# Maxima over the partitions: a GpSimd all-reduce replaced by a trip through DRAM and a VectorE reduction

## The chip, the cores and the metric

The kernel runs on one core of a Trainium2 chip. The metric is the device time in microseconds (us). TensorE does the matrix products (the profile's PE, and PEld for its weight loads), VectorE (DVE), ScalarE (ACT) and GpSimd (POOL) the elementwise work, SyncE (SP) issues DMAs. Each takes its instructions in the order in which they were written; they wait for each other through semaphores.

## The reference

One inference step of a two-layer trunk, for a prompt of 16 + 1024 tokens and eight running sequences of one token each, 1048 columns in all. Cut to what matters here:

```python
def trunk(x, ...):                       # D_MODEL 1024, D_FF 4096
    for i in range(2):
        h = rms_norm(x, norm_mix_pre[i])
        m = ssd_mixer(h, ...) if i == 0 else rglru_mixer(h, ...)
        x = x + rms_norm(m, norm_mix_post[i])
        h = rms_norm(x, norm_ffn_pre[i])
        x = x + rms_norm(sq_relu_mlp(h, w1[i], w2[i]), norm_ffn_post[i])

def ssd_mixer(u, ...):                   # 32 heads of 64 in 8 groups, state 128
    z, xbc, dt = split(u @ w_in)         # 1024 x 6176
    xbc = silu(causal_conv(xbc))         # 4 taps
    y, h = ssd_chunked(...)              # chunks of 128: decay matrix, carried state
    return group_rms_norm((y + D * x) * silu(z)) @ w_out

def rglru_mixer(u, ...):
    gate, xr = split(u @ w_in + b_in)    # 1024 x 2048
    h = scan(a, b)                       # a, b from sigmoids of block products of conv(xr)
    return (h * gelu(gate)) @ w_out + b_out

def sq_relu_mlp(x, w1, w2):
    return relu(x @ w1) ** 2 @ w2
```

All in float32.

## The kernel before, in words

Channels lie on the partitions and the 1048 columns along the free dimension, in pieces of 350, 350 and 348. Each float32 product is made of float16 products: an operand is scaled by a power of two and split into a high and a low half, and three products hi x hi, hi x lo, lo x hi add up in PSUM.

**Weight strips.** The weights come in strips of 128 x 2048 float32 (1 MB; 256 output channels over all 1024 inputs). `load_strip` (L537) has SyncE load a strip into `ws`, which has two buffers. `wconv` (L565) finds the largest magnitude in each partition, `rm` (128x1): with VectorE (L581, L602) or, for the strips of kind "a" in the SSD stage, as a sum of magnitudes with ScalarE (L579). `strip_scale` (L542) makes the maximum over the 128 partitions, in every partition, `wgb`, and from it the power of two (`qw`, `pw`, `sw`, in `pow2`, L529 to L533) and its inverse `winv` (L548). Then `split` (L551) writes the halves: ScalarE the high one (L558), VectorE the low one (L562), into `wh` (five buffers). For strips of kinds "H" and "S", in the FFNs, `sums` makes combinations `wp` as well (L640, L641) and GpSimd forms differences in `ws` in place (L648). 105 strips are scaled on `rm` or its like and four more on `gmx`, maxima taken earlier (L583).

**Stages.** From 100 to 990 us of the profiled execution, the SSD stage: eight groups, and for each the projection of the next one on TensorE (L742, evacuated by ScalarE: `pre` at L1150 and L1155, `z` at L1249) between nine chunk steps (`tp`, L1284; `st`, L1327; `yo`, L1331 and L1335). In each chunk the state goes through GpSimd (`hst`, L1344, times a decay) and VectorE (L1345, plus the new part), GpSimd adds to `yf` (L1352), and the group's norm adds squares there (`gsq`, L1435). SyncE loads the decay factors `L` (L1294) and `ex` (L1299) for each chunk. Then the output projection; from 1190 the first FFN, in Strassen-like units (`unit`, L1618: the products `mm` of L677, added up in `z` by VectorE at L1634 to L1645 and in `acc` at L1565, split into `H` at L1516 or L1598); from 1800 the LRU stage; from 2230 the second FFN.

**Order.** The body writes the program as interleaved generators. After that `Order` builds the graph of all instructions, runs a list schedule over it with a length for each instruction (`Order.length`, L122 on), four rounds forward and back, keeps the best, and pins every engine, SyncE included, to that order. The length of a partition all-reduce stands there as 600 ns.

Of the kernel before, what the change touches and what calls it, by code (L numbers as in the profile page):

```python
# [12 lines left out]
F32 = mybir.dt.float32  # L13
# [3 lines left out]
OP = mybir.AluOpType  # L17
AX = mybir.AxisListType
PSUM = bass.MemoryType.PSUM
DRAM = bass.MemoryType.DRAM  # L20
RED = bass.bass_isa.ReduceOp
EXPSET = "natural_log_exp_and_others"

P = 128
# [55 lines left out]
class Order:  # L80
# [40 lines left out]
    @staticmethod  # L121
    def length(i, kind, outs, ins):  # L122

        n = max([int(np.prod([x[1] for x in list(a.ap)[1:]] or [1])) for a in outs + ins] or [1])
        scal = sum(all(x[1] == 1 for x in list(a.ap)[1:]) for a in ins)
        eng = str(i.engine).split(".")[-1]
        if kind == "InstLoadActFuncSet":
            return 20
        if kind == "InstDMACopy":
            return 350 if eng == "SP" else 600  # L130
        if eng == "PE":
            c = int(np.prod([x[1] for x in list(outs[0].ap)[1:]]))
            if ins[0].dtype == F32:
                t = 2 * max(110, c / 1.2 + 2)
                return t / 2 if tuple(i.tile_size)[1] < 128 else t
            return max(30, c / 2.4 + 2.2)
        if eng == "DVE":
            if kind == "InstReciprocal":
                return 150 + 6 * n
            if "InstTensorScalarPtr" == kind and i.is_tensor_tensor_scan:  # L140
                return 150 + 2.08 * n
            return 65 + n / 0.96 + 65 * min(scal, 2) * (n > 1) + 80 * (len(outs) > 1)
        if eng == "Activation":
            return 90 + 0.83 * n + 90 * scal + 190 * (len(outs) > 1)
        if kind == "InstPartitionAllReduce":
            return 600
        if kind == "InstTensorTensor":
            return 200 + 2.19 * n
        return 110 + 6 * n if kind == "InstTensorCopy" else 110 + n
# [255 lines left out]
class Body:  # L405
# [26 lines left out]
    def setup(self):  # L432
        nc, tc, ctx = self.nc, self.tc, self.ctx
        self.const = ctx.enter_context(tc.tile_pool(name="const", bufs=1))
        self.tiny = ctx.enter_context(tc.tile_pool(name="tiny", bufs=3))
        self.upool = ctx.enter_context(tc.tile_pool(name="u", bufs=1))
        self.ws = ctx.enter_context(tc.tile_pool(name="ws", bufs=2))
        self.wh = ctx.enter_context(tc.tile_pool(name="wh", bufs=5))
# [30 lines left out]
        gb = c.tile([P, 5], F32, name="gb")  # L469
# [18 lines left out]
        self.yd = [self.dram.tile([P, 4 * NV], F16, name=f"yd{i}") for i in range(G)]  # L488
        self.csd = self.dram.tile([288, P], F32, name="csd")
        self.esd = self.dram.tile([288, P], F32, name="esd")  # L490
        self.bcd = [self.dram.tile([8, 2, P], F32, name=f"bcd{i}") for i in range(2)]
        self.mad = [self.dram.tile([P, KT * w], F32, name=f"mad{c}") for c, w in enumerate(WC)]
        a = self.a
# [46 lines left out]
        return st  # L540

    def strip_scale(self, gmax):  # L542
        nc, ty = self.nc, self.tiny
        gb = ty.tile([P, 1], F32, tag="wgb", name="wgb")
        nc.gpsimd.partition_all_reduce(gb, gmax, P, RED.absmax)  # L545
        s, p = self.pow2(gb, 1, ty, "w")
        inv = ty.tile([P, 1], F32, tag="winv", name="winv", bufs=8)
        nc.vector.tensor_scalar(inv, p, 2.0 ** -14, None, op0=OP.mult)  # L548
        return s, inv, gb
# [1382 lines left out]
```

## Time and profile before

| what | value |
|---|---|
| time, median of 3 runs | 2951.6 us (2949.22 to 2952.95) |
| profiled execution | 2956.49 us; span from first to last instruction 2954.8 us |
| granted TensorE clock, mean | 0.950 |
| DMA traffic | 237.73 MB, mean 80 GB/s |
| POOL instructions | 1036 |

In lines of groups, `L545 POOL PARTITION_ALL_REDUCE wgb<-rm x105 | 49.8, 475 | 728.9 <-issue 358.3` reads: line 545, engine, operation, tile written and read, 105 of them, 49.8 us busy in all, 475 ns each, 728.9 us of idle time of the engine just before them, of which "issue" (a wait for nothing that the profile shows) ended 358.3 us. In lines of waits, the engine with its tile and line stands left of the arrow, what it waited for right of it, then us in total, how often, and the longest. In lines in order of time: start, length, engine, line, operation, tiles, shapes, and in brackets the engine's idle time before it and what ended that.

### The profile page before, as it was taken

Reading aid. Unit: us, or ns where it says so; the run is one execution under the profiler, and the core shown is the slowest. Engines: PE = TensorE matmul, PEld = TensorE weight load, DVE = VectorE, ACT = ScalarE, POOL = GpSimd, SP = SyncE. Lnnn points to the kernel's source line nnn. Section 1 sums busy time; section 2 is a strip of 40 time slices with the busy share of each in tenths; the row PEclk is TensorE's granted clock in tenths of the full one; section 3 lists DMA queues with packets and bytes.
Section 4 is the critical chain, followed back from the end, with each engine's and each line's share of the span. In section 5 each row is a group of like instructions: output and inputs, shape, how many; then the busy total and the mean of one; then the engine's idle time right before and its main releaser. Section 6 shows DMA issues by size and latency. Waiting matters only on the chain.

```text
span 2954.8 us, 57301 instructions
## 1 busy us (share of the span) xinstructions
PE 2585.9 (88%) x23193; PEld 2048.1 (69%) x23193; DVE 2089.2 (71%) x4682; ACT 1408.2 (48%) x2436; POOL 764.0 (26%) x1036
## 2 busy tenths in 40 slices
PE   4979889788888998977988899998999879979898
PEld 2656556555555565876988896665667868979886
DVE  4757557656754477676878778896885677778786
ACT  4556455555654345334335144577664335244252
POOL 2222222222222102353232210122112652241211
PEclk9999999899898999998999999999999989999999
DMA  3232333133235522010112112310230011111122
GB/s 123 76 112 80 121 115 116 68 132 103 79 118 182 201 88 68 30 44 30 59 44 87 58 58 97 140 38 33 83 136 30 30 44 44 44 44 44 45 84 91
DMA packets 71498, 237.73 MB, mean 80 GB/s; under 512 B 11120, under 2 KB 37152, under 8 KB 50368
## 3 DMA queue, kind: packets, MB, share of 16 engines
q1 hardware_dynamic: 64848, 199.35, 19.5%
q0 software_dynamic: 6384, 34.71, 3.1%
q8 instruction: 181, 2.97, 0.4%
q14 instruction: 85, 0.70, 0.1%
HBM read 194.67 MB, written 39.36 MB: 79 GB/s over the span
## 4 chain that ended last, share of the span: by engine, by line
DVE 25%; PE 21%; issue 15%; POOL 7%; ACT 4%; DMA 2%; SPq 0%; POOLq 0%; DVEq 0%; ACTq 0%
PE mm L742 17%; DVE wh L562 4%; DVE wp L641 3%; PE mm L677 2%; POOL ws L648 2%; DVE z L1636 2%; DVE z L1640 1%; POOL f L1594 1%; DVE acc L1565 1%; DMA ws<-w 1%; POOL f L1609 1%; DVE z L1637 1%; DVE r L596 1%; DVE H L1516 1%; DVE z L1643 1%
## 5 line engine op out<-in xcount | busy, mean ns | idle before, releaser
L742 PEld LDWEIGHTS <-wh 128*128 128x128 f16 x8832 | 863.3, 99 | 546.7 <-issue 90.0
L742 PE MATMUL mm<-U,wh 128*128 128x350 f16 (+1 forms) x5760 | 912.1, 319 | 74.2 <-ACT z L1249 42.4
L677 PEld LDWEIGHTS <-wh 128*128 128x128 f16 x8640 | 695.8, 100 | 48.0 <-issue 31.2
L677 PE MATMUL mm<-H,wh 128*128 128x175 f16 (+1 forms) x4320 | 385.4, 242 | 24.6 <-DVE z L1640 18.4
L677 PEld LDWEIGHTS <-wp 128*128 128x128 f16 x3888 | 313.0, 99 | 130.5 <-issue 130.2
L648 POOL TENSOR_TENSOR ws<-ws 128x256 f32<-128x256 f32 (+1 forms) x192 | 225.0, 1172 | 318.0 <-DVE wp L641 287.0
L529 DVE TENSOR_SCALAR qw<-wgb 128x1 f32<-128x1 f32 x109 | 16.5, 152 | 356.7 <-POOL wgb L545 356.2
L545 POOL PARTITION_ALL_REDUCE wgb<-rm x105 | 49.8, 475 | 728.9 <-issue 358.3
L677 PE MATMUL mm<-U,wp 128*128 128x175 f16 (+1 forms) x1728 | 157.7, 246 | 84.5 <-DVE z L1634 67.2
L677 PE MATMUL mm<-U,wh 128*128 128x175 f16 (+1 forms) x1728 | 162.6, 246 | 15.4 <-DVE z L1637 10.6
L742 PE MATMUL mm<-H,wh 128*128 128x350 f16 (+3 forms) x1344 | 172.9, 290 | 2.1 <-DVE z L1634 2.1
L677 PE MATMUL mm<-TT,wh 128*128 128x175 f16 (+1 forms) x1728 | 168.9, 251 | 0.0
L558 ACT ACTIVATE wh<-ws,sw 128x2048 f16<-128x2048 f32 (+1 forms) x53 | 104.3, 1968 | 127.4 <-DVE winv L548 85.8
L562 DVE SCALAR_TENSOR_TENSOR wh<-ws,sw,wh 128x1024 f16<-128x1024 f32 (+1 forms) x106 | 139.7, 1347 | 26.9 <-ACT wh L558 26.9
L1552 ACT ACTIVATE z<-z,ti 128x700 f32<-128x700 f32 (+1 forms) x72 | 63.0, 875 | 185.3 <-DVE z L1643 185.3
L1162 DVE SCALAR_TENSOR_TENSOR conv<-pre,ssmall,conv 128x1072 f32<-128x1072 f32 x96 | 133.9, 1396 | 7.0 <-ACT conv L1160 5.1
L1308 ACT ACTIVATE L<-L,cs 128x128 f32<-128x128 f32 (+1 forms) x288 | 89.0, 378 | 96.4 <-DMA L<-csd 89.4
L677 PE MATMUL mm<-H,wp 128*128 128x175 f16 (+1 forms) x864 | 92.0, 244 | 37.6 <-DVE z L1645 23.6
L562 DVE SCALAR_TENSOR_TENSOR wh<-ws,s,wh 128x256 f16<-128x256 f32 x256 | 112.8, 490 | 1.0 <-ACT wh L558 1.0
L558 ACT ACTIVATE wh<-ws,s 128x512 f16<-128x512 f32 x128 | 83.8, 710 | 44.7 <-PE mm L677 22.9
L581 DVE TENSOR_REDUCE rm<-ws 128x1 f32<-128x2048 f32 x41 | 93.4, 2280 | 14.7 <-DMA ws<-w 10.6
L1327 PE MATMUL st<-xdd,Bt 128*128 128x256 f32 (+1 forms) x144 | 49.9, 430 | 59.0 <-ACT Bt L1317 57.7
(281 smaller groups left out, 4385.6 us busy)
## 6 DMA issues: line engine op xcount, KB each, us to landing
ws<-w SPq DMA_DIRECT2D x64, 1024.0 KB, 4.9
ws<-w_ssd_in SPq DMA_DIRECT2D x24, 1024.0 KB, 5.0
L<-csd SPq DMA_DIRECT2D x64, 256.0 KB, 4.3
ws<-w_lru_in SPq DMA_DIRECT2D x12, 1024.0 KB, 4.8
xd<-xc POOLq DMA_DIRECT2D x6, 1400.0 KB, 5.4
xc<-xd SPq DMA_DIRECT2D x6, 1400.0 KB, 5.8
h<-ssd_h SPq DMA_DIRECT2D x8, 1024.0 KB, 4.9
ex<-esd SPq DMA_DIRECT2D x128, 64.0 KB, 3.2
```

What stands on the lines that cost most here:

```text
L558: nc.scalar.activation(w[:, 0, sl], st[:, sl], AF.Copy, scale=s[:, i:i + 1])
L562: nc.vector.scalar_tensor_tensor(w[:, 1, o:o + h], st[:, o:o + h], s[:, i:i + 1], w[:, 0, o:o + h], op0=OP.mult, op1=OP.subtract)
L581: nc.vector.tensor_reduce(rm, st, axis=AX.X, op=OP.max, apply_absolute_value=True)
L641: nc.vector.scalar_tensor_tensor(lo, a, sk, hi, op0=OP.mult, op1=OP.subtract)
L648: tt(o, a, b, op=op)
L677: self.nc.tensor.matmul(ps, l, r, start=n == 0, stop=n == len(ops) - 1)
L742: nc.tensor.matmul(ps, l, r, start=first and i == 0, stop=last and i == n - 1)
L1162: nc.vector.scalar_tensor_tensor(out, pre[:, k:k + E], w4[:, k:k + 1], out, op0=OP.mult, op1=OP.add)
L1308: nc.scalar.activation(L[:Q, h, :Q], L[:Q, h, :Q], AF.Relu, scale=-1.0, bias=self.cs[:Q, tt, 4 * g + h:4 * g + h + 1])
L1327: nc.tensor.matmul(st[:, :256], Bt[:Q], fl(xdd[:Q]), start=True, stop=True)
L1552: nc.scalar.activation(z, z, AF.Relu, scale=ti)
L1636: nc.vector.tensor_tensor(xy, pb, zv[:, 2:3].to_broadcast([P, 2, n]), op=OP.add)
```

## The change

`strip_scale` no longer calls GpSimd. SyncE writes the 128 partition values to a small DRAM tile (one of four in turn), then reads them back as one row spread over all 128 partitions (`wrow`, one buffer), and VectorE takes the maximum of each partition's row into `wgb`. The small tiles have two buffers instead of three. The length of a partition all-reduce in `Order.length` becomes 6200 ns; two such instructions remain, `gb` in `setup` and `gx` in the LRU stage. The list schedule is made anew from the changed graph. Lines behind the new ones in `setup` move down by two, those behind `strip_scale` by eight.

```diff
         if kind == "InstPartitionAllReduce":
-            return 600
+            return 6200
...
-        self.tiny = ctx.enter_context(tc.tile_pool(name="tiny", bufs=3))
+        self.tiny = ctx.enter_context(tc.tile_pool(name="tiny", bufs=2))
...
+        self.mxd = [self.dram.tile([P, 1], F32, name=f"mxd{i}") for i in range(4)]
+        self.nmax = 0
...
     def strip_scale(self, gmax):
+
         nc, ty = self.nc, self.tiny
+        d = self.mxd[self.nmax % 4]
+        self.nmax += 1
+        nc.sync.dma_start(d, gmax)
+        row = ty.tile([P, P], F32, tag="wrow", name="wrow", bufs=1)
+        nc.sync.dma_start(row, d.rearrange("p o -> o p").to_broadcast([P, P]))
         gb = ty.tile([P, 1], F32, tag="wgb", name="wgb")
-        nc.gpsimd.partition_all_reduce(gb, gmax, P, RED.absmax)
+        nc.vector.tensor_reduce(gb, row, axis=AX.X, op=OP.max)
         s, p = self.pow2(gb, 1, ty, "w")
```

How that moves instructions, at three places.

POOL in an SSD group, before. An ISA row that names no tile stands ahead of an instruction of another kind of POOL program; the row with `wgb` is the all-reduce.

```order
L1352 TENSOR_TENSOR yf<-yf,ex 128x2x128
L545 ISA
L545 ISA wgb<-rm 128x1
L1164 COPY cvo<-pre 128x24
L1435 ISA
L1435 TENSOR_TENSOR gsq<-gsq 128x350
L1344 TENSOR_TENSOR hst<-hst,ecd 128x256
```

POOL at the same place now:

```order
L1360 TENSOR_TENSOR yf<-yf,ex 128x2x128
L1172 COPY cvo<-pre 128x24
L1443 TENSOR_TENSOR gsq<-gsq 128x350
L1352 TENSOR_TENSOR hst<-hst,ecd 128x256
L1360 TENSOR_TENSOR yf<-yf,ex 128x2x128
```

The all-reduce and both lone ISA rows are gone; the arithmetic stands in the same order.

VectorE in the first FFN, before, from a strip's maximum to its use (the strip is of kind "H"):

```order
L581 TENSOR_REDUCE rm<-ws 128x1
L1640 TENSOR_TENSOR z<-z,mm 128x2x175
L529 TENSOR_SCALAR qw<-wgb 128x1
L531 TENSOR_SCALAR pw<-qw 128x1
L533 TENSOR_SCALAR sw<-pw 128x1
```

VectorE for the same strip now (L1648 was L1640, L1651 and L1653 were L1643 and L1645, L1573 was L1565, L1642 to L1645 were L1634 to L1637):

```order
L589 TENSOR_REDUCE rm<-ws 128x1
L1648 TENSOR_TENSOR z<-z,mm 128x2x175
L1651 TENSOR_TENSOR z<-z,mm 128x175
L1653 TENSOR_TENSOR z<-z,mm 128x175
L1573 SCALAR_TENSOR_TENSOR acc<-z,iq_15320,acc 128x700
L1642 TENSOR_TENSOR z<-z,mm 128x174
L1644 TENSOR_TENSOR z<-mm,z 128x2x174
L1645 TENSOR_TENSOR z<-z,mm 128x174
L553 TENSOR_REDUCE wgb<-wrow 128x1
L531 TENSOR_SCALAR qw<-wgb 128x1
```

Seven instructions instead of one stand between the maximum of the partitions and the first use of what comes of it.

SyncE at the start, before (`xc` are the columns of x, `ws` the strips, `small` and `ssmall` the small parameters):

```order
L990 DMA xc<-x 128x1050
L449 DMA small<-small 128x232
L990 DMA xc<-x 128x1050
L990 DMA xc<-x 128x350 x2
L539 DMA ws<-w_ssd_in 128x2048 x2
L990 DMA xc<-x 128x6x348
L449 DMA ssmall<-ssmall 128x384
```

SyncE at the start now (`mxd` is the small DRAM tile):

```order
L449 DMA small<-small 128x232
L541 DMA ws<-w_ssd_in 128x2048
L998 DMA xc<-x 128x1050 x2
L998 DMA xc<-x 128x350 x2
L998 DMA xc<-x 128x6x348
L541 DMA ws<-w_ssd_in 128x2048
L449 DMA ssmall<-ssmall 128x384
L1191 DMA cst<-ssd_cst 128x96 x2
L549 DMA mxd_144<-rm 128x1
L998 DMA xc<-x 128x1050 x2
L998 DMA xc<-x 128x700
L998 DMA xc<-x 128x2x348
```

The first strip now stands ahead of x, and the second and third piece of x behind the write of the first maximum. In the FFNs SyncE's rows were weight loads one after another; now each strip has three, its load, the write of its maximum and the read of the row, and the next strip's load stands behind them.

## The prediction

> **What bounds the kernel now.** I read the engine totals first, then the stages, then who waits, then the order in time at two places.
>
> ```profile
> PE 2585.9 (88%) x23193; PEld 2048.1 (69%) x23193; DVE 2089.2 (71%) x4682; ACT 1408.2 (48%) x2436; POOL 764.0 (26%) x1036
> DVE 25%; PE 21%; issue 15%; POOL 7%; ACT 4%; DMA 2%; SPq 0%; POOLq 0%; DVEq 0%; ACTq 0%
> L529 DVE TENSOR_SCALAR qw<-wgb 128x1 f32<-128x1 f32 x109 | 16.5, 152 | 356.7 <-POOL wgb L545 356.2
> L545 POOL PARTITION_ALL_REDUCE wgb<-rm x105 | 49.8, 475 | 728.9 <-issue 358.3
> ...
> q8 instruction: 181, 2.97, 0.4%
> ```
>
> TensorE is nearest to full, yet it stands for 2954.8 - 2585.9 = 369 us. POOL looks almost idle, but 15% of the chain that ended last, some 440 us, is "issue": an engine waited for nothing that the profile shows. The two groups say where: POOL stood 358.3 us on "issue" before all-reduces, and VectorE 356.2 us for their results. By stage (us; TensorE, its weight loads, VectorE, ScalarE, POOL, granted clock):
>
> ```profile
> 0.00:100.00 100.00, 56.85 (x504) 35.75 (x505) 51.90 (x124) 47.97 (x71) 24.77 (x46) 0.93 0.34 123
> 100.00:990.00 890.00, 764.39 (x5094) 514.88 (x5092) 553.44 (x1373) 493.78 (x912) 223.41 (x349) 0.92 0.32 107
> 990.00:1190.00 200.00, 187.25 (x1209) 119.71 (x1207) 135.95 (x285) 88.67 (x152) 28.12 (x48) 0.96 0.32 118
> 1190.00:1800.00 610.00, 527.54 (x6416) 512.22 (x6414) 464.95 (x1092) 235.38 (x412) 197.01 (x235) 0.95 0.16 56
> 1800.00:2230.00 430.00, 418.22 (x2701) 276.07 (x2700) 355.11 (x573) 264.37 (x392) 77.44 (x98) 0.99 0.23 81
> 2230.00:2850.00 620.00, 539.39 (x6457) 518.48 (x6456) 461.16 (x1089) 248.41 (x438) 202.92 (x250) 0.96 0.13 45
> ```
>
> The SSD stage (100 to 990) leaves TensorE idle for 125.6 us, the two FFNs (from 1190 and 2230) for 82.5 and 80.6; the LRU stage is nearly full, at clock 0.99. Where TensorE rests, the clock falls too. The waits that carry it (total, times, longest), TensorE's in the SSD stage, then VectorE's for the maximum in the SSD stage and in each FFN:
>
> ```profile
> PE st L1327 <- ACT Bt L1317: 57.7, 14, 13.5
> PE mm L742 <- ACT z L1249: 42.4, 10, 7.2
> ...
> DVE qw L529 <- POOL wgb L545: 139.3, 13, 15.5
> ...
> DVE qw L529 <- POOL wgb L545: 85.3, 19, 7.7
> ...
> DVE qw L529 <- POOL wgb L545: 91.5, 22, 6.8
> ```
>
> In time, POOL in the SSD stage, what its all-reduce line issues, and VectorE and TensorE at two such places:
>
> ```profile
> 446.05 0.69 POOL L1352 TENSOR_TENSOR yf<-yf,ex 128x256 f32<-128x256 f32 x1 [0.34 <-DVE ex L1351]
> 454.65 0.41 POOL L545 PARTITION_ALL_REDUCE wgb<-rm  x1 [7.91 <-issue]
> 454.94 0.27 POOL L1164 COPY cvo<-pre 128x24 f32<-128x24 f32 x1
> 462.56 1.00 POOL L1435 TENSOR_TENSOR gsq<-gsq 128x350 f32<-128x350 f32 x1 [7.36 <-DVE bc L1387]
> ...
> L545 POOLq MODIFY_POOL_CONFIG  x158: 1/11/37, 31.7 to 2813.6; - x158
> ...
> 420.53 0.15 DVE L529 TENSOR_SCALAR qw<-wgb 128x1 f32<-128x1 f32 x1 [13.66 <-POOL wgb L545]
> ...
> 423.64 6.49 PE L742 MATMUL mm<-U,wh 128*128 128x350 f16 x24 [6.04 <-ACT z L1249]
> ...
> 431.85 3.73 PE L742 MATMUL mm<-U,wh 128*128 128x350 f16 x24
> ...
> 464.31 1.22 PE L1327 MATMUL st<-xdd,Bt 128*128 128x256 f32 x2 [5.21 <-ACT Bt L1317]
> ```
>
> The all-reduce itself lasts 0.41 us. Around it POOL stands 7.9 and 7.4 us: a change of POOL's program to the all-reduce and one back to ordinary arithmetic, each marked by a MODIFY_POOL_CONFIG of at most 37 ns. There are 158; at some 6.6 us they take about 1040 us of POOL (estimate), more than its 764 us of visible work. VectorE, in order, stands at qw (13.66 us at 420), ScalarE behind it, TensorE behind both (to 423.64); at 464.31 TensorE has waited 5.21 us, just behind the change that ended at 462.56. And after 6.04 us of rest the same 24 matmuls take 6.49 instead of 3.73 us, so a rest costs nearly 3 us more than its length. The Trainium skill ("GPSIMD Engine Reference", Instruction dispatch) says that the first call into a newly loaded POOL routine pays about 6 us with no visible instruction; the trace agrees.
>
> **The change, part by part.** *Removed:* 109 all-reduces, and with them the program changes: in the order, POOL's ISA rows that name no tile, which stand ahead of each change, fall from 165 to 7. The end feels this only where someone waited.
>
> SSD stage: the two TensorE waits sum to 100.1 us, and the lowered clock costs 764.4 x (1 - 0.92) = 61 us, together 161. Both rests shown in time ended in a program change or in qw. I take two thirds, 107 us: the strip still has to wait for its maximum, only by another way.
>
> FFNs: TensorE's rests are 163 us, and the clocks of 0.95 and 0.96 cost 26 + 22 us, together 211. VectorE's 85.3 + 91.5 us at qw lie just ahead of them. I take half, 105 us, for the reason of the next part.
>
> *Added, per strip:* a write of 128x1 to DRAM, a read of 128x128 back, a reduction. The nearest rows (KB each, us to landing; then two issues of SyncE of which the second needs the first landed):
>
> ```profile
> ws<-w SPq DMA_DIRECT2D x64, 1024.0 KB, 4.9
> ...
> ex<-esd SPq DMA_DIRECT2D x128, 64.0 KB, 3.2
> ...
> wab<-w_ab SPq DMA_DIRECT2D x8, 128.0 KB, 2.2
> ...
> cst<-ssd_cst SPq DMA_DIRECT2D x8, 48.0 KB, 5.2
> ...
> L<-csd SPq DMA_DIRECT2D x8, 4.0 KB, 1.5
> ...
> 147.70 0.34 SPq L1363 DMA_DIRECT2D bcd<-row  x1
> ...
> 149.69 0.59 SPq L1366 DMA_DIRECT2D bc<-bcd  x1
> ...
> L581 DVE TENSOR_REDUCE rm<-ws 128x1 f32<-128x2048 f32 x41 | 93.4, 2280 | 14.7 <-DMA ws<-w 10.6
> ```
>
> A small write and the read that needs it stand 1.99 us apart; the 64 KB read, spread over partitions as the new one is, lands after 3.2. The reduction of 128 columns lies between qw's 0.15 and 2280/16 + 150 ns = 0.29; I take 0.25. The trip is 2.0 + 3.2 + 0.25 = 5.4 us. Ends: 1.5 + 2.2 + 0.15 = 3.9 below; above 5.2 + 4.9 + 0.3 = 10.4, where both queue behind a weight load. I take 5.4, since two of its three rows are of the same kind. The Trainium skill ("DMA: Bandwidth & Descriptors", Anatomy of one DMA) gives about 2.0 us fixed per DMA plus bytes; by it the trip would be an estimated 4.4 us, and the sum by half of 1 us for each of the 64 FFN strips, 32 us, better.
>
> *Moved:* the new order leaves more work on VectorE between a maximum and its use. At the H strip shown, one instruction stood there (L1640); now seven:
>
> ```profile
> 1486.87 0.51 DVE L1640 TENSOR_TENSOR z<-z,mm 128x348 f32<-128x348 f32 x1
> 1487.49 0.34 DVE L1643 TENSOR_TENSOR z<-z,mm 128x174 f32<-128x174 f32 x1
> ...
> 1488.11 0.94 DVE L1565 SCALAR_TENSOR_TENSOR acc<-z,iq,acc 128x696 f32<-128x696 f32 x1
> ```
>
> Two like the first, four like the second, one like the third: 2 x 0.51 + 4 x 0.34 + 0.94 = 3.3 us of cover. A trip of 5.4 leaves VectorE standing about 2.1 us, where it stood 85.3/19 = 4.5 and 91.5/22 = 4.2 us. So about half of that wait goes, hence the half above. At 3.9 nearly all goes (211 us gained); at 10.4 the wait is 7 us, longer than now.
>
> *VectorE* gets 109 x 0.25 = 27 us of work. It lies in VectorE's free time (553 of 890 us busy in the SSD stage, 465 of 610 in an FFN); were that cover gone, 27 us.
>
> *SyncE* carries 218 more issues, and while a read waits for its write, some 2 us, every load behind it waits too. The 109 x 64 KB are 7 MB of the 237.7 that the DMA engines move at a 13 to 34% share (the next to last column of the stages): 0. In the FFNs the next weight load now stands behind the maximum's trip, but had to wait for its buffer anyhow:
>
> ```profile
> SPq L539 <- DVE wh L562: 1787.0, 99, 41.3
> ```
>
> 18 us each time, so 5 us of trip are hidden. In the SSD stage the loads of decay factors stand behind it; that is one reason for two thirds. At the start x now comes after a weight strip, and more x behind the first maximum: +5 us, the length of one weight load. The other stages: -5, of 24.5 us that TensorE rests between 990 and 1190 and from 1800 to 2230. Two copies of the small tiles instead of three, and one of wrow: 0, since a strip's small tiles are used up before the strip after the next needs them; were one held, it would show as the wait on the trip priced above.
>
> *The length of 6200 instead of 600 ns* now bears on two all-reduces only (gb, gx): 0 by itself, since the order is made anew in any case; were it made worse, it would be the small gain below.
>
> *Sum:* -107 - 105 + 5 - 5 = -212 us. The profiled execution took 2956.5 us, 4.9 above the median of the runs (0.17%); from the median, 2951.6 - 212 = 2740 us.
>
> **Rivals.** *Small gain (2810 to 2945).* VectorE's order becomes the bound in the FFNs: 465 us plus strips' reductions in 610 leaves little slack when the stage shortens, and TensorE's rests there all end on VectorE. For it: covers of 3.3 us against 5.4. Then only the SSD gain stays: 2951.6 - 107 = 2845 us.
>
> *Everything goes (2580 to 2680).* Trip near 3.9 us, TensorE as in the LRU stage: -161 - 211 = 2580 us. For it: the LRU row with 418.22 of 430 at 0.99. Against it: VectorE is 76% busy in an FFN before the stage shortens.
>
> *Slower.* The reduction was cheapest where it was: 0.41 us in place against two DMAs through SyncE, which goes in order. Place: the strips' trips, written and read between weight loads. Price: each us by which a trip exceeds 5.4 and that reaches TensorE costs 109 us; the gain of 212 is gone at 2 us more, a trip of 7.4 with nothing hidden. At 8 us it is 2951.6 - 212 + 2.6 x 109 = 3023 us. For it: the 5.2 us row and SyncE's long waits. Against it: the order puts each trip ahead of the next weight load, and the DMA engines are mostly free. The Trainium skill ("GPSIMD Engine Reference", Engine selection) names GpSimd for reductions over partitions and advises against VectorE, so by that rule this one would win. In the trace the program change, not the reduction, is what POOL's all-reduce costs.
>
> **How the numbers follow.** Forecast (2680 to 2810): 0.55. Small gain: 0.20. Everything goes: 0.14. Slower: 0.07. The new wait just eats the gain: 0.04. The predicted time is 2740 us. The range takes the forecast, the better half of the small gain and most of the last good case: 2640 to 2870 us. 0.2%, 6 us, is about what a measurement here can tell from no change. Faster 0.89, within 0.2% 0.04, slower 0.07.
>
> **What would show it.** q8's bytes fall from 2.97 MB to some 0.2; "issue" nearly leaves POOL's waits and the chain; the 57.7 and 42.4 us of TensorE fall under a third each; VectorE waits for wrow instead of wgb, about 2 us a strip, 100 to 200 us in all; the granted clock in the SSD stage rises above 0.95. I am wrong if the read of wrow lands after 8 us, if SyncE's loads of L or ex grow late in the SSD stage, or if VectorE's wait there stays above 4 us a strip.

## The result, and the profile after

The changed kernel takes 3270.0 us (median of 4 runs, 3262.7 to 3281.0) against 2950.4 us (2947.4 to 2953.0) on the same chip: ratio 1.109, 95% interval 1.105 to 1.113. It is 320 us slower; the forecast was 212 us less. The profiled execution took 3281.0 us, its span 3279.2 us, at a granted clock of 0.906 (0.950 before).

From the page of the changed kernel: engine totals, the chain that ended last by engine and by line, the group of the new reduction (busy us, mean ns | idle us before it and its releaser), and queue 8 (packets, MB).

```profile
PE 2672.0 (81%) x23193; PEld 2112.5 (64%) x23193; DVE 2135.6 (65%) x4791; ACT 1407.4 (43%) x2436; POOL 716.9 (22%) x927
...
q8 instruction: 181, 2.97, 0.6%
...
DMA 40%; DVE 30%; PE 14%; ACT 8%; issue 6%; POOL 1%; SPq 0%; DVEq 0%; ACTq 0%; POOLq 0%
DMA mxd<-rm 22%; DMA wrow<-mxd 11%; PE mm L750 10%; DVE wh L570 4%; DVE wp L649 3%; DVE rm L589 2%; DMA ws<-w 2%; PE mm L685 2%; ACT wh L566 2%; DMA L<-csd 1%; ACT wh L587 1%; DVE z L1644 1%; DVE r L604 1%; DVE ss L784 1%; DMA ex<-esd 1%
...
L553 DVE TENSOR_REDUCE wgb<-wrow 128x1 f32<-128x128 f32 x109 | 31.0, 285 | 723.8 <-DMA wrow<-mxd 723.8
```

DMA was 2% of the chain and is 40%, and a third of the whole chain is two transfers: the write of 512 bytes and the read of them. VectorE stands 724 us before 109 reductions that last 31 us together. POOL's 7% have become 1% and the 15% of "issue" 6%: most of what the change set out to remove is gone.

The stages (same columns as in the prediction; SSD, then the two FFNs, whose borders have moved), and VectorE's wait for the row in each of the three:

```profile
100.00:990.00 890.00, 776.22 (x5132) 516.60 (x5131) 567.13 (x1406) 495.69 (x913) 215.61 (x320) 0.93 0.36 111
...
1200.00:1930.00 730.00, 563.33 (x6434) 547.69 (x6433) 475.04 (x1102) 237.51 (x416) 179.88 (x210) 0.88 0.15 48
...
2440.00:3180.00 740.00, 579.45 (x6547) 554.77 (x6547) 481.21 (x1131) 251.57 (x445) 193.76 (x227) 0.88 0.12 41
```

```profile
DVE wgb L553 <- DMA wrow<-mxd: 126.8, 13, 16.9
...
DVE wgb L553 <- DMA wrow<-mxd: 211.2, 24, 13.0
...
DVE wgb L553 <- DMA wrow<-mxd: 225.2, 26, 11.7
```

The SSD stage does about the same work in the same 890 us: the new wait of 126.8 us took the place of the old one of 139.3, and others came with it. TensorE's waits in this stage, VectorE's for `ex` and SyncE's ahead of the row's reads (total us, times, longest):

```profile
PE yo L1343 <- DVE L L1326: 33.3, 9, 9.2
PE yo L1339 <- DVE ex L1359: 30.1, 17, 4.9
PE st L1335 <- ACT Bt L1325: 25.2, 14, 5.1
...
DVE ex L1359 <- DMA ex<-esd: 30.7, 8, 5.6
...
SPq L551 <- DMA mxd<-rm: 233.5, 27, 13.1
```

Before, TensorE waited 57.7 us for `Bt`, VectorE never for the load of `ex`, and of the other two there was less:

```profile
PE yo L1335 <- DVE L L1318: 15.3, 4, 7.0
PE yo L1331 <- DVE ex L1351: 1.9, 2, 1.0
```

SyncE now stands ahead of each row's read, and `ex` is loaded by SyncE behind it. Each FFN needs 730 to 740 us for what took 610 to 620, and the LRU stage between them 510 (1930 to 2440) for 430: 120 + 120 + 80 = 320 us, the whole loss. In the LRU stage VectorE's wait for the row is 82.3 us, where it waited 12.4 for the all-reduce. In an FFN TensorE now rests 167 and 161 us instead of 83 and 81, and the clock falls from 0.95 and 0.96 to 0.88.

The DMA view (KB each, median us from issue to landing), and what SyncE waited for (total us, times, longest):

```profile
ws<-w_ssd_in SPq DMA_DIRECT2D x24, 1024.0 KB, 11.6
...
ex<-esd SPq DMA_DIRECT2D x128, 64.0 KB, 3.3
...
wrow<-mxd SPq DMA_DIRECT2D x109, 64.0 KB, 4.5
...
mxd<-rm SPq DMA_DIRECT2D x105, 0.5 KB, 8.1
```

```profile
SPq L551 <- DMA mxd<-rm: 836.9, 103, 13.1
```

Half a kilobyte lands later than the megabyte of a weight strip did in the profile before (4.9 us). The earliest of the 109 writes lands after 6.9 us, so it is no queue that is sometimes full. The strips of the SSD stage (`w_ssd_in`) land later too, after 11.6 us where it was 5.0. One strip of the first FFN on the chain, start and length in us:

```profile
1512.68 11.08 PE mm L685 x126
1523.80 0.52 DVE z L1644
...
1524.59 2.29 DVE rm L589
1526.90 10.03 DMA mxd<-rm
...
1536.99 3.18 DMA wrow<-mxd
...
1540.20 0.30 DVE wgb L553
...
1541.98 0.44 DVE z L1648
1542.46 11.54 PE mm L685 x126
```

This is a ring of 29.8 us (1512.68 to 1542.46): a strip's maximum per partition, write, read, reduction; behind the reduction in VectorE's fixed order stands `z` L1648, which empties TensorE's accumulators; then 126 matmuls; then the `z` ahead of the next strip's maximum. VectorE and TensorE take turns. VectorE's rows inside it (start, length, idle before):

```profile
1529.68 0.34 DVE L1645 TENSOR_TENSOR z<-z,mm 128x174 f32<-128x174 f32 x1
1540.20 0.29 DVE L553 TENSOR_REDUCE wgb<-wrow 128x1 f32<-128x128 f32 x1 [10.19 <-DMA wrow<-mxd]
```

The cover that the prediction counted, 3.3 us, is there (1526.79 to 1530.02); the trip is 13.3 us up to the reduction (1526.90 to 1540.20).

### The profile page after: what moved, and what is told of

Read it like the earlier page. It is cut to its first block, busy times and chain, and to the rows that moved or that the text cites. A ratio compares the mean times of both kernels' runs of the same rounds, so it can differ in the third digit from the quotient of the medians.

```text
span 3279.2 us, 57342 instructions
## 1 busy us (share of the span) xinstructions
PE 2672.0 (81%) x23193; PEld 2112.5 (64%) x23193; DVE 2135.6 (65%) x4791; ACT 1407.4 (43%) x2436; POOL 716.9 (22%) x927
## 3 DMA queue, kind: packets, MB, share of 16 engines
q8 instruction: 181, 2.97, 0.6%
## 4 chain that ended last, share of the span: by engine, by line
DMA 40%; DVE 30%; PE 14%; ACT 8%; issue 6%; POOL 1%; SPq 0%; DVEq 0%; ACTq 0%; POOLq 0%
DMA mxd<-rm 22%; DMA wrow<-mxd 11%; PE mm L750 10%; DVE wh L570 4%; DVE wp L649 3%; DVE rm L589 2%; DMA ws<-w 2%; PE mm L685 2%; ACT wh L566 2%; DMA L<-csd 1%; ACT wh L587 1%; DVE z L1644 1%; DVE r L604 1%; DVE ss L784 1%; DMA ex<-esd 1%
## 5 line engine op out<-in xcount | busy, mean ns | idle before, releaser
L750 PEld LDWEIGHTS <-wh 128*128 128x128 f16 x8832 | 867.7, 100 | 532.4 <-issue 44.9
L685 PEld LDWEIGHTS <-wh 128*128 128x128 f16 x8640 | 723.2, 102 | 228.6 <-issue 202.4
L553 DVE TENSOR_REDUCE wgb<-wrow 128x1 f32<-128x128 f32 x109 | 31.0, 285 | 723.8 <-DMA wrow<-mxd 723.8
L685 PE MATMUL mm<-H,wh 128*128 128x175 f16 (+1 forms) x4320 | 410.8, 251 | 100.1 <-DVE z L1648 81.9
L685 PEld LDWEIGHTS <-wp 128*128 128x128 f16 x3888 | 345.2, 105 | 108.2 <-issue 107.9
L685 PE MATMUL mm<-U,wh 128*128 128x175 f16 (+1 forms) x1728 | 171.7, 254 | 119.1 <-DVE z L1648 99.2
L685 PE MATMUL mm<-U,wp 128*128 128x175 f16 (+1 forms) x1728 | 165.8, 257 | 47.4 <-DVE z L1651 35.3
L570 DVE SCALAR_TENSOR_TENSOR wh<-ws,sw,wh 128x1024 f16<-128x1024 f32 (+1 forms) x106 | 136.7, 1320 | 30.7 <-ACT wh L566 30.6
L1316 ACT ACTIVATE L<-L,cs 128x128 f32<-128x128 f32 (+1 forms) x288 | 88.8, 378 | 92.0 <-DMA L<-csd 85.4
L648 ACT ACTIVATE wp<-ws,s 128x128 f16<-128x128 f32 x144 | 45.9, 388 | 173.7 <-DVE s L618 173.7
L648 ACT ACTIVATE wp<-ws,sq 128x512 f16<-128x512 f32 x72 | 46.9, 710 | 139.9 <-DVE sq L632 63.4
## 6 DMA issues: line engine op xcount, KB each, us to landing
ws<-w_ssd_in SPq DMA_DIRECT2D x24, 1024.0 KB, 11.6
```

Source lines behind the costliest of these rows:

```text
L570: nc.vector.scalar_tensor_tensor(w[:, 1, o:o + h], st[:, o:o + h], s[:, i:i + 1], w[:, 0, o:o + h], op0=OP.mult, op1=OP.subtract)
L648: nc.scalar.activation(hi, a, AF.Copy, scale=sk)
L685: self.nc.tensor.matmul(ps, l, r, start=n == 0, stop=n == len(ops) - 1)
L750: nc.tensor.matmul(ps, l, r, start=first and i == 0, stop=last and i == n - 1)
L1316: nc.scalar.activation(L[:Q, h, :Q], L[:Q, h, :Q], AF.Relu, scale=-1.0, bias=self.cs[:Q, tt, 4 * g + h:4 * g + h + 1])
```

## The experiments

The kernel before ran beside every group of runs: 2945.3, 2945.8, 2944.9 and 2946.1 us.

### The write by itself

The first run is a chain of transfers alone. Each kind of write of f32 from 128 partitions (or fewer) is followed by a read back and two VectorE instructions that the next one waits for; each round has a read of a 64 KB row besides (`rowt`):

```diff
+        sp(pk4, src[:, 0:1])
+        settle(pk4)
+        sp(p64[:, 0:1], src[:, 0:1])
+        settle(p64)
```

> Leaves the whole computation out: only a chain of DMAs, each one landing before the next is issued, eight of each kind. Theory A (the packed line): the write of 128 values of 4 bytes into one run of 512 bytes lands only after 7 to 8 us also when nothing else moves, and the same write into a column with a pitch of 512 bytes lands in 2 to 3 us; a whole 512-byte row from one partition in about 2 us. Theory B (the number of 4-byte elements): packed and pitched writes both take 7 to 8 us. Theory C (traffic in the kernel): all take about 2 us here, and the 8 us of the changed kernel come from what runs beside. The read of a 64 KB row spread over partitions: 3.0 to 3.5 us in all three.

Measured (304 us in all). The read's issue needs the write landed, so the distance of a pair of issues is the write's time. In order: 128 x 4 bytes packed, 4 bytes at pitch 64, 4 bytes at pitch 512, 32 bytes packed, 512 bytes each, one packet of 512 bytes, 32 x 4 bytes packed.

```profile
40.59 0.34 SPq L1854 DMA_DIRECT2D rowt<-full  x1
40.98 0.42 SPq L1839 DMA_DIRECT2D pk<-src  x1
48.81 0.32 SPq L1831 DMA_DIRECT2D back<-pk  x1
...
51.82 0.32 SPq L1841 DMA_DIRECT2D p<-src  x1
53.27 0.32 SPq L1831 DMA_DIRECT2D back<-p  x1
...
66.90 0.23 SPq L1849 DMA_DIRECT2D one<-src  x1
68.03 0.23 SPq L1831 DMA_DIRECT2D back<-one  x1
```

7.83 us packed, 1.45 at pitch 64, 1.13 as one packet; over the eight rounds 6.9 to 7.8, 1.4 to 1.6 and 1.1. The others: 1.4 to 1.7 at pitch 512, 1.4 to 1.5 for 32 bytes packed, 1.5 to 1.6 for 512 bytes each, 2.9 to 3.2 for 32 elements packed. So neither the 128 packets nor their 4 bytes are slow: it is small pieces side by side. 32 of them cost 2.9 - 1.45 = 1.5 us more, 128 cost 6.2: 46 and 48 ns each. The packed write did not run alone here: the row's read was issued some 0.4 us from it in every round, and how long that read took is not recorded. Theory C, other traffic, is left to the second probe, in which nothing runs beside the write.

A second probe looks for the distance at which this ends:

```diff
+    for e in (1, 2, 4, 8):
+        for pitch in (1, 2, 4, 8, 16):
+            if pitch >= e:
+                ts[e, pitch] = D(f"e{e}p{pitch}", pitch)
...
+            sp(d[:, 0:e], src[:, 0:e])
+            sp(back[:, :pitch], d)
```

> No trunk is computed: 14 kinds of write of 128 partitions, elements of 1, 2, 4 or 8 f32 at pitches of 4 to 64 bytes, five times each, each followed by a read back and a copy. In the first probe 128 x 4 bytes packed took 7.8 us from issue to the read's issue, 32 x 4 bytes packed 3.1 us, and 4 bytes at pitch 64, 32 bytes packed, and one packet of 512 bytes 1.1 to 1.5. Theory A1 (writes below some size that fall into one 64-byte piece of DRAM are done one after another): 4 bytes at pitch 64 takes 1.5 us, at pitch 32, 16 and 8 more in steps towards 7.8. Rival A2 (each element below 32 bytes costs for itself, wherever it falls): pitch 4 to 32 all take about 7.8 us and 8- and 16-byte elements the same; the fast pitch of 64 bytes speaks against it.

Its second round, 4-byte elements at pitches of 4, 8, 16, 32 and 64 bytes:

```profile
81.48 0.32 SPq L1835 DMA_DIRECT2D e1p<-src  x1
88.95 0.32 SPq L1836 DMA_DIRECT2D back<-e1p  x1
...
92.30 0.32 SPq L1835 DMA_DIRECT2D e1p<-src  x1
96.07 0.32 SPq L1836 DMA_DIRECT2D back<-e1p  x1
...
98.43 0.32 SPq L1835 DMA_DIRECT2D e1p<-src  x1
99.89 0.32 SPq L1836 DMA_DIRECT2D back<-e1p  x1
```

7.47, 3.77 and 1.46 us, then 1.63 and 1.47. Over five rounds: pitch 4 took 6.9 to 7.5, pitch 8 3.5 to 4.0, pitch 16 1.4 to 1.5. Elements of 8 bytes packed took 2.6 to 2.8, of 16 bytes packed 1.4 to 1.5. So the packed write is as late with nothing beside it, and theory C is out. Both new theories miss: 4-byte elements are quick from a distance of 16 bytes on (against A2, and earlier than the 64 of A1), and at a distance of 8 bytes elements of 4 bytes take longer than those of 8, so distance is not all.

The DMA engines' share around the packed write of the third round, issued at 147.54 and landed by 154.77 (window, its length, VectorE's and POOL's work, clock, DMA share, GB/s):

```profile
148.10:148.90 0.80, 0.00 (x0) 0.00 (x0) 1.00 0.10 1
148.90:154.70 5.80, 0.00 (x0) 0.00 (x0) 1.00 0.00 0
```

The engines are done with the packets 1.4 us after the issue; in the 5.8 us that follow they do nothing, and the write has not landed. The delay lies behind them, and what takes this time for each piece was not seen.

### The same kernel, the maxima apart

```diff
-        self.mxd = [self.dram.tile([P, 1], F32, name=f"mxd{i}") for i in range(4)]
+        self.mxd = [self.dram.tile([P, P], F32, name=f"mxd{i}") for i in range(4)]
...
-        nc.sync.dma_start(d, gmax)
+        nc.sync.dma_start(d[:, 0:1], gmax)
...
-        nc.sync.dma_start(row, d.rearrange("p o -> o p").to_broadcast([P, P]))
+        nc.sync.dma_start(row, d[0:1, :].to_broadcast([P, P]))
```

The row that is read holds one partition's maximum only, so this kernel does not compute the maximum; it does the same work. It ran first by itself and then four times:

> The changed kernel with one difference: each maximum goes to its own row of a 128x128 DRAM tile (pitch 512 bytes), and the read takes the tile's first row, so it carries only one partition's maximum. Same instructions, same bytes read, same waits. Theory A: the write lands in 2 to 3 us, VectorE's wait for wrow falls from 724 us to below 300, and the time falls to 2800 to 2950 us. Theory B: the write still lands after 8 us, time within 1.5% of 3270. Theory C: as B.

> The pitched kernel again, for an interval: each maximum is written 512 bytes from the next, and the row that is read carries one partition's maximum only. From its first profile 2598 us. Theory A: 2590 to 2610 us, so the pitch alone is worth 660 to 680 us against the changed kernel. The rest against the kernel without any maximum over the partitions (2563 us) is the trip when it lands in 1.4 + 2.9 us: 35 us.

2598.3 us, some 200 less than theory A expected; then 2595.0 (2592.0 to 2600.2), ratio to before 0.881 (0.878 to 0.883), clock 0.994. In the timed run's profile:

```profile
wrow<-mxd SPq DMA_DIRECT2D x109, 64.0 KB, 2.8
...
mxd<-rm SPq DMA_DIRECT2D x105, 0.5 KB, 1.4
...
L555 DVE TENSOR_REDUCE wgb<-wrow 128x1 f32<-128x128 f32 x109 | 30.7, 281 | 115.9 <-DMA wrow<-mxd 115.9
```

The write lands after 1.4 instead of 8.1 us, the read after 2.8 instead of 4.5, VectorE waits 116 instead of 724 us. The two kernels have the same instructions, except for four small writes that fill the DRAM tiles at the start, and their transfers are told the same latencies; the pitch is worth 3270 - 2595 = 675 us. The list schedule came out a little different, with some nine in ten of VectorE's instructions in the same sequence; the share of that is not known, but a change of order no smaller was worth 69 us (below). The strips of the SSD stage land after 5.2 us again. The trip is 8.5 us shorter, so one us of trip costs 675 / 8.5 = 79 us of time, 0.73 us per strip.

### What the maximum costs at all, and where

No maximum over the partitions:

```diff
-        d = self.mxd[self.nmax % 4]
...
-        nc.vector.tensor_reduce(gb, row, axis=AX.X, op=OP.max)
+        gb = gmax
```

> The changed kernel without any maximum over the partitions (each partition is scaled by its own): no all-reduce, no trip. Theory trip (the long trip ate the gain): 2600 to 2750 us, since the reload of POOL's program is gone too and nothing takes its place; my sum for that was 2951 - 372 = 2580 to 2951 - 212 = 2740. Rival theory order (the new list order or the two small buffers are at fault): it stays above 2950 us.

2563.2 us (2560.4 to 2565.1), ratio 0.871 (0.868 to 0.872), below the range of theory trip and far from theory order. The kernel before therefore paid 2945 - 2563 = 382 us for its maxima, the pitched trip pays 32.

The same, with the all-reduces running on GpSimd for nobody, and told as 600 ns again:

```diff
+        gb = gmax
+        gx = ty.tile([P, 1], F32, tag="wgx", name="wgx")
+        nc.gpsimd.partition_all_reduce(gx, gmax, P, RED.absmax)
```

> The kernel without any maximum over the partitions in the chain (each partition scales by its own), and 109 all-reduces still run on GpSimd whose result nobody reads, modelled at 600 ns. Against the 2563 us of the same kernel without them this prices GpSimd's time apart from VectorE's wait for its result. If the program changes hold up GpSimd's other work on the path (as the prediction had it, half of its 212 us): 2650 to 2760 us. If only the wait for the maximum counted: within 20 us of 2563.

2806.6 us (2801.5 to 2814.2), ratio 0.954 (0.951 to 0.956): above both expectations. What POOL waited for before the all-reduces and before its own work:

```profile
POOL wgx L549 <- issue: 117.3, 19, 8.7
POOL hst L1348 <- issue: 103.3, 14, 8.4
```

So 2806.6 - 2563.2 = 243 us of the 382 come with nobody waiting for the result: POOL's time itself, with the changes of its program holding up `hst` and other work behind them. The other 2945 - 2807 = 139 us are, by difference and with the order made anew, the wait for the result.

And the kernel before, its order made for a late maximum:

```diff
         if kind == "InstPartitionAllReduce":
-            return 600
+            return 6200
```

> The kernel before, all-reduce on GpSimd kept; only the length in the list schedule's model goes from 600 to 6200 ns, so that the order is made for a late maximum. If the order alone was what the kernel before lost by (as it was for the changed kernel, where told latencies took 514 us off), VectorE's 356 us of waiting for the all-reduce fall below 150 and the time comes to 2650 to 2800 us. If GpSimd itself is the limit there (its 109 all-reduces, each with a change of program before and after), the time stays within 100 us of the kernel before, 2850 to 3000 us.

2878.7 us (2873.6 to 2879.7), ratio 0.978 (0.976 to 0.979). VectorE's wait:

```profile
DVE qw L529 <- POOL wgb L545: 134.9, 35, 16.1
```

The wait fell from 356 to 135 us, the time only by 66: GpSimd itself is the limit there, as the second expectation had it.

### The slow write kept, the order told of it

The list schedule gives each transfer 2.0 us. First a run that takes over only the other line of the next one:

```diff
+        if len(ap) == 2 and ap[0][1] == 2 and ap[0][0] == 3 * ap[1][1]:
+            idx = np.arange(idx[0], idx[-1] + 1)
```

> The changed kernel, with only the other line of the run with told latencies: the schedule takes two pieces that one access reads with a gap between them as one range (stricter order, same work, latencies of 2.0 us as in the changed kernel). If the told latencies alone took the 514 us off, this one stays within 2% of the changed kernel, 3200 to 3340 us, and VectorE waits about 724 us for the row. If the stricter order had a share in it, it comes out below 3100 us.

Then with the lengths told:

```diff
-                    self.lat[n] = 2000
+                    self.lat[n] = {'mxd': 8000, 'wro': 4200}.get(a.tensor.name[:3], 2000)
```

> The changed kernel with its slow write kept, and the list schedule told how late the two transfers land (8.0 and 4.2 us in place of 2.0 each). Theory 'trip' (the lateness itself cannot be covered: each strip's weights wait for it and there is too little other VectorE work): VectorE still waits over 500 us for the row and the time stays above 3100 us. Rival 'order' (the trip would be bearable, but VectorE's fixed order had placed the reduce some 4 us too early, so that all work behind it stood still): the wait falls below 250 us and the time comes to 2650 to 2800 us, below the kernel before.

With the stricter order alone 3201.1 us (3195.9 to 3202.4), ratio 1.086 (1.084 to 1.089). With the lengths told 2756.1 us (2754.2 to 2761.6), ratio 0.935 (0.933 to 0.938). VectorE's wait in the one and in the other:

```profile
DVE wgb L555 <- DMA wrow<-mxd: 688.1, 93, 18.7
```

```profile
DVE wgb L555 <- DMA wrow<-mxd: 136.5, 23, 14.5
```

The lengths told take 445 us off with the same slow transfers (the stricter order had 69, a share that the expectation did not give it). In the first FFN, from the end of a strip's `rm` to its reduction, the changed kernel has 13.7 us with 3.8 us of VectorE's work in them (medians of 25 strips); here it has 15.3 us with 12.3 us of work (24 strips). "Trip" falls and "order" holds: the lateness could be covered, and the order had covered about the 2 + 2 us that it believed in. What is left against the pitched kernel, 161 us, was not taken apart.

### Other ways to the maximum

TensorE transposes: one f32 matmul with the identity puts all partitions' maxima into each partition's row of an accumulator, and VectorE reduces that.

```diff
-        nc.sync.dma_start(d, gmax)
...
+        t = "cb" if len(self.mmtags) == 4 else self.mmtags[self.mmi % 8]
+        ps = self.psp.tile([P, 512], F32, tag=t, name="mx")
+        nc.tensor.matmul(ps[:, :P], gmax.to_broadcast([P, P]), self.ident, start=True, stop=True)
...
+        nc.vector.tensor_reduce(gb, ps[:, :P], axis=AX.X, op=OP.max)
```

(The small tiles have three buffers again, the stricter order is in, and no strip is prepared while the accumulators are held over split matmuls.)

> The maximum by TensorE and VectorE: one float32 matmul of the maxima, broadcast along the free dimension, with the identity puts all 128 into every partition of a PSUM tile, and VectorE reduces that; three small buffers again. No DMA, no all-reduce. Trip: one matmul of some 0.4 us and a reduction of 0.3 us in place of 12.7 us, so within 2% of the run without a maximum, 2620 to 2770 us. Rival theory order: above 2950 us, and VectorE waits at the maximum for TensorE's queue.

2693.2 us (2690.1 to 2696.1), ratio 0.915 (0.913 to 0.917): within the range expected, but 5% above the run without a maximum, not 2%. VectorE waits only 22.7 us for the new matmuls; where the rest of these 130 us lies was not taken apart.

Four pieces of 128 bytes in place of 128 of 4: VectorE transposes inside blocks of 32 partitions first.

```diff
-        self.mxd = [self.dram.tile([P, 1], F32, name=f"mxd{i}") for i in range(4)]
+        self.mxd = [self.dram.tile([4, 32], F32, name=f"mxd{i}") for i in range(4)]
...
-        nc.sync.dma_start(d, gmax)
+        tr = ty.tile([P, 32], F32, tag="wtr", name="wtr")
+        nc.vector.transpose(tr, gmax.to_broadcast([P, 32]))
+        nc.sync.dma_start(d, tr[0:P:32, :])
```

> The changed kernel with the same maximum written as four pieces of 128 bytes in place of 128 of 4: VectorE turns the maxima within each block of 32 partitions (one more instruction of 128x32), SyncE writes partitions 0, 32, 64 and 96 to the 512 bytes in DRAM, and the row is read back as before. Theory A (what cost the time is the write of 128 elements of 4 bytes into 512 adjacent bytes, which lands after 8.1 us): this write lands after 1.1 to 1.6 us, VectorE's wait for the row falls from 724 us to about 115, and the time is 2600 to 2620 us, the pitched run's 2598 and some us for 109 more VectorE instructions of about 0.1 to 0.2 us. Rival (the pitched kernel was fast for another cause, its DRAM places lying apart or its row not waiting for all partitions): a packed 512-byte line would still land late, and the time stays above 3000 us.

And with the two transfers told as 2.5 and 3.5 us, and the stricter order:

> The kernel that writes four pieces of 128 bytes, and the list schedule told 2.5 and 3.5 us for the two transfers in place of 2.0 each, somewhat above the 1.5 and 2.8 us of its chain. If its last 65 us against the pitched kernel are reduces placed too early (VectorE waited 156 us for the row): 2595 to 2630 us. If they are VectorE's added 22 us and another order: 2640 to 2680 us.

2660.1 us (2651.0 to 2662.1), ratio 0.902 (0.899 to 0.904), and with the lengths told 2620.1 us (2615.4 to 2621.4), ratio 0.890 (0.889 to 0.891). On the chain of the first:

```profile
1510.70 1.53 DMA mxd<-wtr
1512.29 2.79 DMA wrow<-mxd
```

The same 512 adjacent bytes land after 1.5 us, as theory A had it; the time came out 40 us above what was expected, of which 109 transposes of 0.205 us are 22. The told lengths and the stricter order together took 40 us off, within the first expectation. 2620 us is the fastest kernel here that computes the whole maximum: 325 us below the kernel before, 650 below the changed one.

## Why the prediction was wrong

**The step that failed: the price of the trip.** Its first row was the wrong kin. The 1.99 us between `bcd<-row` and `bc<-bcd` are those of a write of 8 KB in long pieces; the new one has 4-byte pieces side by side, and took 8.2 us (6.9 to 13.9). I called the two rows "of the same kind" by their size and direction, and the shape of the pieces decided. The read took 4.5 us, not 3.2, the reduction 0.285, not 0.25: 13.0 us against 5.4, and beyond the upper end of 10.4, which allowed for queueing behind a weight load and not for the shape. With pieces apart the trip measures 1.4 + 2.8 + 0.28 = 4.5 us, between the lower end and the value taken. The Trainium skill ("DMA: Bandwidth & Descriptors", Anatomy of one DMA) has a fit for transfers that GpSimd issues, and the estimated 4.4 us worked out from it for these of SyncE agrees with that trip and not with the packed one. Its Specifications section says that transfers below 512 bytes are done as read-modify-write; it names no price, and 4 bytes at a pitch of 16 bytes or more took 1.4 us here.

**The cover was right, and it showed the loss.** 3.3 us of cover were read from the order; 3.8 stand there in the median. By the same step, 13.0 less 3.8 is 9.2 us of standing per strip, and 211.2 / 24 = 8.8 were measured. The sentence "at 10.4 the wait is 7 us, longer than now" had the right sign for the FFNs. What it lacked is why the cover was 3 to 4 us: the schedule believed in 2.0 us for each transfer and left just that room. I costed the order as if its room were given; with the room made for the real lengths, the slow trip gives 2756 us.

**The slower rival was the one that came.** It had the direction and the place, at a chance of 0.07, and its sum, so much for each us of a longer trip, is of the right kind. Its reason was not what came: the reduction was not cheapest where it was, and two DMAs through SyncE are no loss by themselves, since the same two with their pieces apart give 2595 us. Its price, 109 us for each us of trip, is measured as 79; by its own sum 13.0 us would have been 2951.6 - 212 + 7.6 x 109 = 3568 us, 298 too many. What spoke against it in the text, mostly free DMA engines and a place ahead of the next weight load, was true (DMA share 0.12 and 0.15 in the FFNs) and beside the point: a write can land late with nothing in its way.

**What goes with the all-reduces** was right in kind and too small. Waits of POOL for "issue" fell from 358 us before `wgb` alone to 7.3 in all. With 2563 us without any maximum, 382 us were there to be had, not the 212 that were taken nor the 372 (2951.6 - 2580) of "everything goes". My fractions of two thirds and half stood for a trip that would hide only in part; with the pitched trip 350 of the 382 come. The 6.6 us for each program change is POOL's mean wait put down to "issue" before (669.7 us in 102 waits); of the 1040 us estimated from it, 243 reached the end.

**The SSD stage.** Forecast -107 us, measured about nothing: VectorE's wait there is 126.8 us, 13 times, where it was 139.3 us, 13 times, and the clock 0.93 instead of the forecast "above 0.95". TensorE's two waits did fall, from 57.7 to 25.2 us and from 42.4 to nothing, but 33.3 us for `L` and 30.1 for `ex` stand there now. That is 75 us less at the old places and 46 more at the new (15.3 and 1.9 stood there before). The loads behind the trip were a reason for two thirds; `ex` bears it out, while for `L` late loads are not shown, since ScalarE waits 85.4 us for them and waited 89.4. In the pitched kernel the clock is 0.99, and TensorE's waits for `L` and `ex` in the same window are 0.7 and 6.9 us.

**Small points.** VectorE's added work: 27 us forecast, 31.0 measured. VectorE's waits for `wrow`: 100 to 200 us forecast, 723.8 measured. SyncE was to stand some 2 us while a read waits for its write: 836.9 / 103 = 8.1. The length of 6200 ns was costed at nothing, and the two tile copies too; neither was tried by itself in the changed kernel, but both stand in the pitched one too, at 2595 us, so they are not the loss. In the kernel before the length was worth 66 us, because there it bears on all 109. Of the wrong signs named at the end, the first came in another place: the read of the row lands after 4.5 us, and the write ahead of it after 8. The second came: the transfer of `ex` itself is as quick as before (3.3 us, 3.2), but VectorE waits for it 30.7 us in the SSD stage, where it never did. So did the third: 126.8 us over the 28 maxima of that stage are 4.5 us a strip.

**q8** was a wrong reading. Its bytes were to fall from 2.97 to 0.2 MB; they are the same 2.97 MB in 181 packets with and without the all-reduces. The changes of POOL's program left the waits and not this queue, so they are not what it carries.

## What to carry to other kernels

Before you price a small transfer by its bytes, look at its pieces: many of 4 or 8 bytes side by side land late, and a pitch of 16 bytes, or a transpose that makes longer pieces, buys it back. Where an order is fixed by a model, its guess for a latency is the room that it leaves: the same slow transfer cost 445 us more with 2.0 us believed than with its real length. And price what a wait removes and what the work itself occupies apart: here 139 and 243 us.

## What the runs showed of the hardware

A write of 128 elements of 4 bytes into 512 adjacent bytes of DRAM landed after 6.9 to 7.5 us with nothing else running (in one such write the last 5.8 us found the DMA engines idle); at a pitch of 8 bytes 3.5 to 4.0, at 16 bytes and more 1.4 to 1.7, once 2.1; 32 elements packed 2.9 to 3.2; 8-byte elements packed 2.6 to 2.8; 16-byte ones 1.4 to 1.5. The read of the row just behind such a write took 4.5 us in the changed kernel and 2.8 behind a quick one; whether it is the write or the fuller wait of SyncE that delays it was not tried. Strips of 1 MB in the SSD stage landed after 11.6 us (median) in the changed kernel and after 5.2 with the maxima apart.

The Trainium skill ("GPSIMD Engine Reference", Engine selection) sends reductions over partitions to GpSimd. For 128 x 1 values, 109 times among GpSimd's other work, three ways around it were faster here: 2693 us by TensorE, 2660 and 2620 by a short write, against 2945.
